# Decoder step on one core: sample queries' memory logits moved from TensorE to GpSimd products and VectorE sums, and a third of the early weight splits moved to GpSimd

## The chip, the core and the metric

The kernel runs on one core of one Trainium2 chip. A core has a matrix engine (TensorE, PE in the profile), a vector engine (VectorE, DVE), a scalar engine (ScalarE, ACT), GpSimd (POOL) and SyncE (SP), which here issues nearly all the DMAs. Each works through its own row of instructions in order and waits for the others by semaphores. Matmul results go to PSUM; all else lies in SBUF. The metric is the device time of one launch in microseconds (us), median of the runs. A change of under 0.2%, 3.3 us here, is about what a measurement of this kernel can't tell from no change.

## The reference, cut to what matters

One layer of a decoder with three parallel branches, for a prompt of 256 tokens and for 8 samples of 4 new tokens each (32 rows), with the same weights. The branch that the change touches is the cross attention of the samples' queries into cached memory keys, 4 heads of 128, 256 keys for each sample:

```python
def memory_attend(q, k, v):
    s = jnp.einsum('bqhd,bmhd->bhqm', q, k).astype(jnp.float32) * (HEAD_DIM ** -0.5)
    p = jax.nn.softmax(s, axis=-1)
    return jnp.einsum('bhqm,bmhd->bqhd', p.astype(v.dtype), v)
...
qm = rms_norm(q_mem.reshape(b, t, MEM_HEADS, HEAD_DIM), p['g_q_mem'])
y_mem = memory_attend(qm, mem_k, mem_v).reshape(b, t, MEM_WIDTH) @ p['w_mem_out']
```

For the samples `mem_k` is `cache_mem_k`, an input. All arithmetic is in float32.

## The kernel before

All weights stand in one array, the wall, as 504 slabs of 128 partitions x 1024 numbers (512 KB), in the order in which they are used. Each slab is loaded by SP into a buffer `wr` (4 of them), rounded by ScalarE to a high half `wh` in the fast matmul format (line 305), and VectorE subtracts that from the original to get the low half `wl` (line 316, "the split"). There are 4 buffers of `wh` and `wl`. TensorE then does, for the 8 blocks of a slab, three products of 128x128 by 128x288: high by high and low activations, low by high activations (`products`, line 488): 24 matmuls a slab. The 288 columns are 256 prompt tokens and 32 sample rows.

The order of the work on each engine is written when the program is built: every piece of work is a generator that asks for an engine for so many us; a planner (`Order.run`) takes the ask that can start first, by rank where several can, and issues the instructions in that order. Its costs are the functions `dve`, `act`, `pool`, `pe`, `sp`, and nothing is reordered at run time. `main` gives the order of the slabs: memory projection (slabs 0 to 15), the first convolution tiles (16 to 23), the other convolution tiles (24 to 31), the four memory-query heads (`mem_head`, 32 to 39), the eight stick-breaking heads (40 to 87), then gates and branch projections, the output and the MLP.

Of the samples' memory attention (`samples`): the queries of all four heads are spread by VectorE into a zeroed tile `qmx` of 32 columns for each head and sample, so that each sample's columns are zero outside its own four rows. Eight loads bring the keys `mkc`, transposed on the host, 512 KB for each sample. TensorE multiplies in 32 steps (line 1033) and adds all up in one PSUM tile `zm` (128 rows: head x sample row; 256 keys). Softmax and the products with the values follow, then the stick-breaking samples (`sb_sample`).

GpSimd has little to do before: it zeroes tiles, multiplies the convolution windows of the samples (line 706, 992 elements, four times), and in the last two thirds adds and squares tiles of 288 columns (lines 1332 and 1346). VectorE also runs the convolution's 31 taps for each of four tiles (line 719), the norms of the heads (lines 814 to 832, 434 to 438) and the splits of activations (843).

Of the kernel before, what the change touches and what calls it, by code (L numbers as in the profile page):

```python
# [14 lines left out]
P = 128  # L15
# [136 lines left out]


def dve(n, *flags, **take):
    return Ask("DVE", 0.18 + n / 920.0, flags, **take)


def act(n, *flags, **take):
# [17 lines left out]
PAD = 64  # L176
SHIFT = 5
VISIT, VISIT_K = 4, 8
MM = 0.131
MM_MEM = 0.226  # L180

# [2 lines left out]
def tile_decoder_step(ctx: ExitStack, tc: tile.TileContext, xT, memT, wall, cvec, kmat, ptab,  # L184
# [124 lines left out]
    def sub_part(s, i):  # L309
        sl = slabs[s]  # L310
        n = SLAB // sl.parts
        yield dve(n, late=Order.HOP + 0.1)
        if i == 0:
            sl.l = shifted("wl", s)
        c = slice(i * n, (i + 1) * n)
        nc.vector.tensor_sub(sl.l[:, c], sl.raw[:, c], sl.h[:, c].bitcast(F32))  # L316
        done(sl.split[i])
        if i == sl.parts - 1:
            give("wr")
# [559 lines left out]
    qmx = []  # L879

    def mem_head(h):
        def evac(ps):
            box = []
            yield from head_norm(ps, C_GQM, box, Flag())
            q = box[0]
            if h == 0:
                yield pool(1024, k4=1)
                qmx.append(tl("k4", [P, MH, NB, NS]))
                nc.gpsimd.memset(qmx[0], 0.0)
            yield dve(NS, *([qm_made[0]] if h else []))  # L890
            spread(nc, qmx[0][:, h], q[:, NP:])
# [12 lines left out]
            yield pe(0.5, pa=1)  # L904
            tp = bank("pa")
            for m in range(2):
                for a in range(2):
                    nc.tensor.transpose(tp[:, m * NP + a * P:m * NP + (a + 1) * P],  # L908
                                        p[:, a * ML + m * P:a * ML + (m + 1) * P], ident)
# [90 lines left out]
    def sample_values(load, aex, psum, x_T, new, first, cost):  # L1000
# [18 lines left out]
            give("k4")  # L1019
        give("k4", 2)  # L1020

    def samples():

        tiles, flags = [], [Flag() for _ in range(NB)]
        yield sp(qm_made[0])
        add(load_tiles(mem_tiles(mkc, [P, MH, ML]), tiles, flags, range(NB)), 2)
        for b in range(NB):
            if b % VISIT_K == 0:
                yield pe(VISIT_K * 0.5, *flags[b:b + VISIT_K], *qm_made, **({} if b else {"pl": 1}))
            if b == 0:  # L1030
                zm = bank("pl")[:, :ML]
            for h in range(MH):
                nc.tensor.matmul(zm[h * NS:(h + 1) * NS, :], qmx[0][:, h, b, :], tiles[b][:, h, :],  # L1033
                                 start=(b == 0), stop=(b == NB - 1))
            give("k4")
        give("k4")
        yield dve(0, *om_made, s=1)
        p = tl("s", [P, 512])[:, :ML]
        yield from softmax_rows(zm, 1, p)
        give("pl")  # L1040
# [372 lines left out]
    def main():  # L1413
        yield from warm_up()
        yield from mem_products()
        yield from conv_products([evac_lin(0, "pa"), evac_gat(0, "pa"), evac_lin(1, "pm"), evac_gat(1, "pm")])
        for j in range(2, CT):
            yield from main_tile(hx, evac_lin(j, "pm"))
            yield from main_tile(hx, evac_gat(j, "pm"))
        add(samples(), 3.0)  # L1420
        for h in range(MH):
            yield from main_tile(hx, mem_head(h), 2 + 0.05 * h)
        for h in range(SH):
            yield from main_tile(hx, sb_key(h), 2.2 + 0.05 * h)
            yield from main_tile(hx, sb_query(h), 2.2 + 0.05 * h)
# [55 lines left out]
def _layout(inp):  # L1481
# [38 lines left out]
    for k2 in range(KT // 2):  # L1520
        r = slice(2 * k2 * P, (2 * k2 + 2) * P)
        put_rows(np.concatenate([w_in[r, j * P:(j + 1) * P] for j in (0, CT, 1, CT + 1)], 1))
    for j in range(2, CT):
        put(w_in, j)
        put(w_in, CT + j)
    for h in range(MH):
        put(w_in, m0 + h)
    for h in range(SH):
        put(w_in, k0 + h)
        put(w_in, q0 + h)  # L1530
# [12 lines left out]
    for c in range(4):  # L1543
# [30 lines left out]
    n_pool = a["cache_sb_k"].shape[1]  # L1574
    ck = a["cache_sb_k"][0].reshape(n_pool, P, 2, 4, HD)
    cvv = a["cache_sb_v"][0].reshape(n_pool, P, 2, 4, HD)
    return {
        "xT": feat(x),
        "memT": feat(a["mem_prompt"][0]),
# [6 lines left out]
        "mkc": np.ascontiguousarray(a["cache_mem_k"][0].transpose(0, 3, 2, 1)),  # L1586
# [34 lines left out]
```

## Time and profile before

| what | us |
|---|---|
| median of 3 timed runs (1635.0 to 1635.33) | 1635.23 |
| profiled execution, first to last instruction | 1632.5 |
| TensorE busy | 1627.7 |
| VectorE busy | 992.1 |
| ScalarE busy | 739.3 |
| GpSimd busy | 139.1 |

The profiled execution is known by its span; the page gives no other time of its own for it. Engines' busy times overlap and don't add up. In the rows below, a group is written as line, engine, operation, tile written <- tiles read, shapes and count, then busy us, mean ns of one, and the idle time before it with what ended it; a row of the timeline or of the chain begins with its start and length in us from the start of the span. A tile that is called `k` in the profile is one of the pool `k4` (9 tiles of 1024 columns). `pm`, `pa` and `pl` are PSUM tiles.

### The profile page before, as it was taken

The numbers are of one execution on the slowest core, as the hardware profiler recorded it, in microseconds if no ns is written. First come the engines' busy times: TensorE is split into PE (matmuls) and PEld (weight loads), VectorE is DVE, ScalarE is ACT, GpSimd is POOL, SyncE is SP. The second block draws the span as 40 slices with busy tenths as digits, with TensorE's granted clock in tenths as the row PEclk, the third lists the DMA queues.
The fourth block names the chain that finished last, engine by engine and source line by source line (L and its number), as shares of the span: only waits on it lengthen the run. The fifth ranks groups of instructions, "written<-read, shape, count | busy, mean of one in ns | idle before, by whom it ended". The sixth has DMA issues, their size and how long they took to land.

```text
span 1632.5 us, 30962 instructions
## 1 busy us (share of the span) xinstructions
PE 1627.7 (100%) x12786; PEld 1610.3 (99%) x12786; DVE 992.1 (61%) x1471; ACT 739.3 (45%) x1070; POOL 139.1 (9%) x104
## 2 busy tenths in 40 slices
PE   9999999999999999999999999999999999999999
PEld 7999999999999999999999999999999999999999
DVE  8889888877677655565555544455445554455443
ACT  8746766644444534444443333333333333333332
POOL 0020000000000000001222200121001210022100
PEclk9999999999999999999999999999999999999999
DMA  9787465777755555546655555555555555555563
GB/s 339 217 186 251 153 209 189 248 257 252 254 166 169 163 179 167 174 153 212 191 176 168 169 168 168 169 169 174 165 173 170 168 170 169 168 168 168 180 194 99
DMA packets 107103, 305.39 MB, mean 187 GB/s; under 512 B 19922, under 2 KB 29522, under 8 KB 106962
## 3 DMA queue, kind: packets, MB, share of 16 engines
q1 hardware_dynamic: 106818, 303.39, 58.2%
q8 instruction: 100, 1.64, 0.4%
q14 instruction: 41, 0.34, 0.1%
q10 hardware_dynamic: 144, 0.02, 0.0%
HBM read 297.05 MB, written 6.32 MB: 186 GB/s over the span
## 4 chain that ended last, share of the span: by engine, by line
PE 99%; DMA 0%; SPq 0%; ACT 0%; DVE 0%; issue 0%
PE pm L488 93%; PE pm L541 3%; PE pa L488 1%; PE pl L1017 1%; PE pl L1190 0%; PE pa L854 0%; PE pa L855 0%; PE pa L853 0%; DMA wr<-in_wall 0%; PE pl L1033 0%; PE pa L827 0%; PE pa L1144 0%; PE pa L908 0%; PE pa L1141 0%; PE pa L1143 0%; PE pa L1107 0%
## 5 line engine op out<-in xcount | busy, mean ns | idle before, releaser
L305 ACT CAST wh<-wr 128x1024 fp32r<-128x1024 f32 (+1 forms) x520 | 530.3, 1022 | 648.1 <-PE pm L488 597.0
L488 PE MATMUL pm<-a,wh 128*128 128x288 f32 x5184 | 739.1, 293 | 0.0
L316 DVE TENSOR_TENSOR wl<-wr,wh 128x1024 fp32r<-128x1024 f32 (+1 forms) x520 | 617.2, 1190 | 195.2 <-ACT wh L305 190.5
L488 PEld LDWEIGHTS pm<-a,wh 128*128 128x128 f32 x5184 | 696.7, 188 | 1.3 <-issue 1.2
L488 PE MATMUL pm<-a,wl 128*128 128x288 f32 x2592 | 397.0, 292 | 0.0
L488 PEld LDWEIGHTS pm<-a,wl 128*128 128x128 f32 x2592 | 358.4, 188 | 0.0
L488 PE MATMUL pm<-k,wh 128*128 128x288 f32 x2160 | 306.7, 292 | 0.0
L488 PEld LDWEIGHTS pm<-k,wh 128*128 128x128 f32 x2160 | 290.2, 188 | 0.0
L488 PE MATMUL pm<-k,wl 128*128 128x288 f32 x1120 | 171.6, 292 | 0.0
L488 PEld LDWEIGHTS pm<-k,wl 128*128 128x128 f32 x1120 | 155.1, 188 | 0.0
L1346 POOL TENSOR_TENSOR t<-t 128x288 f32<-128x288 f32 x64 | 96.7, 1511 | 599.5 <-DVE t L1343 599.5
L1360 DVE TENSOR_TENSOR a<-a,pm 128x288 f32<-128x288 f32 x64 | 29.0, 454 | 122.4 <-PE pm L488 122.4
L1343 DVE SCALAR_TENSOR_TENSOR t<-pm,rx 128x288 f32<-128x288 f32 x64 | 29.2, 457 | 90.4 <-PE pm L488 90.4
L1349 ACT CAST k<-t 128x288 fp32r<-128x288 f32 x56 | 24.1, 433 | 115.6 <-POOL t L1346 115.6
L1262 DVE TENSOR_TENSOR t<-pm,rx 128x288 f32<-128x288 f32 x48 | 22.0, 458 | 71.5 <-PE pm L488 71.5
L488 PE MATMUL pm<-s,wh 128*128 128x288 f32 x400 | 65.1, 292 | 0.0
L719 DVE SCALAR_TENSOR_TENSOR a<-a,cv,a 128x256 f32<-128x256 f32 x120 | 57.5, 480 | 1.4
L1332 POOL TENSOR_TENSOR t<-t,t 128x288 f32<-128x288 f32 x15 | 21.6, 1441 | 419.3 <-ACT t L1329 419.3
L488 PEld LDWEIGHTS pm<-s,wh 128*128 128x128 f32 x400 | 56.6, 188 | 0.0
L1351 DVE TENSOR_TENSOR k<-t,k 128x288 fp32r<-128x288 f32 x52 | 23.8, 458 | 51.1 <-ACT k L1349 51.1
L541 PE MATMUL pm<-wh,a 128*128 128x512 f32 x128 | 34.6, 391 | 0.2 <-ACT wh L305 0.2
L488 PE MATMUL pm<-s,wl 128*128 128x288 f32 x160 | 33.8, 292 | 0.0
(212 smaller groups left out, 784.4 us busy)
## 6 DMA issues: line engine op xcount, KB each, us to landing
wr<-in_wall SPq DMA_DIRECT2D x488, 512.0 KB, 3.6
wr<-in_wall SPq DMA_DIRECT2D x32, 256.0 KB, 4.8
k<-in_kpool SPq DMA_DIRECT2D x32, 256.0 KB, 5.9
k<-in_vpool SPq DMA_DIRECT2D x32, 256.0 KB, 5.8
k<-in_mkc SPq DMA_DIRECT2D x8, 512.0 KB, 10.2
k<-in_mvc SPq DMA_DIRECT2D x8, 512.0 KB, 6.5
t<-in_xT SPq DMA_DIRECT2D x16, 144.0 KB, 3.7
out_yT<-a SPq DMA_DIRECT2D x16, 144.0 KB, 1.9
```

The lines of the kernel that those rows point to most:

```text
L305: nc.scalar.copy(sl.h[:, c], sl.raw[:, c])
L316: nc.vector.tensor_sub(sl.l[:, c], sl.raw[:, c], sl.h[:, c].bitcast(F32))
L488: nc.tensor.matmul(ps, w, a, start=(first and i == 0), stop=(last and i == len(todo) - 1))
L541: nc.tensor.matmul(ps[m], y[:, m * P:(m + 1) * P], z[:, w], start=(k == 0 and j < 2), stop=(k == KT - 1 and j in (4, 5)))
L719: nc.vector.scalar_tensor_tensor(c[:, :NP], up[:, k:k + NP], w, c[:, :NP], op0=ALU.mult, op1=ALU.add)
L1262: nc.vector.tensor_mul(g, ps, rx)
L1332: nc.gpsimd.tensor_add(sq_sum[0], sq_sum[0], res[0])
L1343: nc.vector.scalar_tensor_tensor(r, ps, 0.0, r2, op0=ALU.max, op1=ALU.mult)
L1346: nc.gpsimd.tensor_mul(r, r, r)
L1349: nc.scalar.copy(a.h, r)
L1351: nc.vector.tensor_sub(a.l, r, a.h.bitcast(F32))
L1360: nc.vector.tensor_add(x1[j], x1[j], ps)
```

## The change

Four things change.

1. The samples' logits leave TensorE. The keys now lie with 128 partitions of (sample, a quarter of 32 keys, head): `lane_loads` brings 8 tiles of 128 x 8 x 128, 512 KB each, of which the first two are loaded at once and each further one when the tile two before it is used up. `lane_queries` copies the queries on GpSimd to a tile in which each query row stands four times, TensorE transposes it four times, ScalarE copies it out of PSUM. `lane_products` multiplies on GpSimd each key tile by each of the four queries (32 products of 1024 elements), and for each product VectorE sums over the 128 elements of a head (`lane_sum`); a product waits for the sum two before it. `lane_rows` brings the logits back into the former layout by VectorE transposes of 32 x 32 blocks.
2. Of the slabs 24, 27, ... 108 (`LENT`, 29 of them) GpSimd makes the low half instead of VectorE.
3. The memory-query heads come before the convolution tiles 2 and 3, in the program and in the wall.
4. The planner's costs of VectorE and GpSimd are changed. With all this the planner makes a new order for every engine.

The diff, cut:

```diff
 def dve(n, *flags, **take):
-    return Ask("DVE", 0.18 + n / 920.0, flags, **take)
+    return Ask("DVE", 0.17 + n / 1004.0, flags, **take)
...
 def pool(n, *flags, **take):
-    return Ask("POOL", 0.3 + n / 420.0, flags, **take)
+    return Ask("POOL", 1.0 + n / 580.0, flags, **take)
...
+LANES = 8
+LENT = range(24, 110, 3)
...
     def sub_part(s, i):
         sl = slabs[s]
         n = SLAB // sl.parts
-        yield dve(n, late=Order.HOP + 0.1)
+        other = s in LENT
+        yield (pool if other else dve)(n, late=Order.HOP + 0.1)
...
-        nc.vector.tensor_sub(sl.l[:, c], sl.raw[:, c], sl.h[:, c].bitcast(F32))
+        (nc.gpsimd if other else nc.vector).tensor_sub(sl.l[:, c], sl.raw[:, c], sl.h[:, c].bitcast(F32))
...
-            if h == 0:
-                yield pool(1024, k4=1)
-                qmx.append(tl("k4", [P, MH, NB, NS]))
-                nc.gpsimd.memset(qmx[0], 0.0)
-            yield dve(NS, *([qm_made[0]] if h else []))
-            spread(nc, qmx[0][:, h], q[:, NP:])
+            yield act(NS)
+            nc.scalar.copy(qs[:, h, :], q[:, NP:])
...
+    def lane_loads(cache, tiles, got, used):
+        for c in range(LANES):
+            yield sp(*([used[c - 2]] if c >= 2 else []), k4=1)
+            t = tl("k4", [P, LANES, HD])
+            nc.sync.dma_start(t, cache[c])
...
+    def lane_queries(q, made, x):
+        yield pool(512, *made, s=1)
...
+        nc.gpsimd.tensor_copy(x[0].rearrange("p q (r a) -> p q r a", a=4), v)
+        yield pe(0.45, pa=1)
+        tp = bank("pa")
+        for i in range(NQ):
+            nc.tensor.transpose(tp[:, i * HD:(i + 1) * HD], x[0][:, i, :], ident)
+        yield act(512)
+        nc.scalar.copy(x[0].rearrange("p q d -> p (q d)"), tp)
...
+    def lane_sum(prod, out, flag):
+        yield dve(LANES * prod.shape[-1])
+        nc.vector.reduce_sum(out, prod, axis=AX.X)
+        give("k4")
+        done(flag)
...
+        for c in range(LANES):
+            for q in range(NQ):
+                yield pool(1024, got[c], *flags[-2:-1], k4=1)
+                prod = tl("k4", [P, LANES, HD])
...
+                nc.gpsimd.tensor_mul(prod, tiles[c], y)
...
+                add(lane_sum(prod, part, flags[-1]), 1.5)
+            give("k4")
+            done(used[c])
...
+    def lane_rows(z, out):
+        yield dve(ML, a=1)
+        t = tl("a", [P, T])[:, :ML]
+        nc.vector.transpose(t, z)
...
-        add(load_tiles(mem_tiles(mkc, [P, MH, ML]), tiles, flags, range(NB)), 2)
-        for b in range(NB):
...
-            for h in range(MH):
-                nc.tensor.matmul(zm[h * NS:(h + 1) * NS, :], qmx[0][:, h, b, :], tiles[b][:, h, :],
-                                 start=(b == 0), stop=(b == NB - 1))
...
+        add(lane_loads(mkc, tiles, got, used), 2)
+        yield from lane_queries(qs[:, :MH, :].rearrange("p h r -> p (h r)"), qm_made, x)
+        yield from lane_products(tiles, got, used, x[0], out)
+        yield from lane_rows(out[0], out)
...
+        add(samples(), 3.0)
+        for h in range(MH):
+            yield from main_tile(hx, mem_head(h), 2 + 0.05 * h)
         for j in range(2, CT):
             yield from main_tile(hx, evac_lin(j, "pm"))
             yield from main_tile(hx, evac_gat(j, "pm"))
-        add(samples(), 3.0)
-        for h in range(MH):
-            yield from main_tile(hx, mem_head(h), 2 + 0.05 * h)
```

The lines after line 178 move: what was line 316 is 321, 706 is 711, 719 is 724, 814 to 832 are 819 to 837. The new order is shown at three places; a row is line, operation, tile written <- tiles read, size, and a number in a tile's name is its serial number.

**VectorE, around slabs 46 and 47.** Before, ten rows in which the splits (L316) of slabs 47, 48 and 49 stand:

```order
L316 TENSOR_TENSOR wl_2092<-wr_1918,wh_2032 128x1024
L1472 COPY k_296_1773<-a_2075 128x8x4
L824 TENSOR_TENSOR t_1992<-t_1991,t_1992 64x288
L814 TENSOR_TENSOR t_2115<-pm_1927,rx 128x288
L316 TENSOR_TENSOR wl_2126<-wr_1955,wh_2083 128x1024
L862 TENSOR_REDUCE sm_108<-pa_2103 128x2
L864 TENSOR_SCALAR sm_108<-sm_108 128x2
L843 TENSOR_TENSOR a_2113<-a_2075,a_2112 128x256
L820 TENSOR_TENSOR t_2116<-t_2116 64x288
L316 TENSOR_TENSOR wl_2172<-wr_2021,wh_2162 128x1024
```

Now, the first passage of the prediction, with the splits (L321) of slabs 46 and 47:

```order
L1046 TENSOR_REDUCE a_1892<-k_350_2032 128x8
L915 TENSOR_TENSOR s_2069<-pa_2052,s_2068 128x512
L825 TENSOR_TENSOR t_2058<-t_2058 64x288
L321 TENSOR_TENSOR wl_2100<-wr_1997,wh_2082 128x1024
L1046 TENSOR_REDUCE a_1892<-k_361_2072 128x8
L829 TENSOR_TENSOR t_2059<-t_2058,t_2059 64x288
L929 TENSOR_TENSOR a_2128<-pa_2111,a_2127 128x256
L819 TENSOR_TENSOR t_2151<-pm_2034,rx 128x288
L321 TENSOR_TENSOR wl_2156<-wr_2002,wh_2130 128x1024
L825 TENSOR_TENSOR t_2152<-t_2152 64x288
L724 SCALAR_TENSOR_TENSOR a_1338<-a_1249,cv,a_1338 128x256
L867 TENSOR_REDUCE sm_108<-pa_2165 128x2
```

The sums L1046 have come between, and every third split has gone. L915, L929 and L819 read PSUM; L825, L829, L724 and the splits read SBUF tiles alone.

**VectorE, around slabs 52 and 53.** Before:

```order
L316 TENSOR_TENSOR wl_2368<-wr_2164,wh_2343 128x1024
L870 RECIPROCAL sm_110<-sm_109 128x2
L824 TENSOR_TENSOR t_2317<-t_2316,t_2317 64x288
L814 TENSOR_TENSOR t_2402<-pm_2291,rx 128x288
L719 SCALAR_TENSOR_TENSOR a_1426<-a_1356,cv,a_1426 128x256 x3
L1129 SCALAR_TENSOR_TENSOR s_2381<-s_2379,s_2380 128x384
L1131 TENSOR_TENSOR s_2381<-s_2381,km 128x2x128
L820 TENSOR_TENSOR t_2403<-t_2403 64x288
L316 TENSOR_TENSOR wl_2460<-wr_2177,wh_2434 128x1024
```

Now, the second passage of the prediction:

```order
L825 TENSOR_TENSOR t_2402<-t_2402 64x288
L819 TENSOR_TENSOR t_2437<-pm_2345,rx 128x288
L321 TENSOR_TENSOR wl_2449<-wr_2299,wh_2390 128x1024
L321 TENSOR_TENSOR wl_2465<-wr_2311,wh_2423 128x1024
L724 SCALAR_TENSOR_TENSOR a_1338<-a_1249,cv,a_1338 128x256
L1186 SCALAR_TENSOR_TENSOR s_2434<-s_2432,s_2433 128x384
L1046 TENSOR_REDUCE a_1892<-k_437_2460 128x8
L1188 TENSOR_TENSOR s_2434<-s_2434,km 128x2x128
L829 TENSOR_TENSOR t_2403<-t_2402,t_2403 64x288
L825 TENSOR_TENSOR t_2438<-t_2438 64x288
L1159 TENSOR_TENSOR a_2522<-pm_2442,rx 128x288
L1046 TENSOR_REDUCE a_1892<-k_442_2496 128x8
```

Two splits now stand one behind the other, with one sum between the taps and the stick-breaking head's rows, and another at the end.

**GpSimd, same part of the program.** Before, the convolution's four products and memsets are all that stands there:

```order
L706 TENSOR_TENSOR k_245_1427<-a_1341,cv 128x992
L706 TENSOR_TENSOR k_251_1465<-a_1343,cv 128x992
L706 TENSOR_TENSOR k_256_1497<-a_1396,cv 128x992
L687 MEMSET a_1562 128x30
L706 TENSOR_TENSOR k_279_1648<-a_1552,cv 128x992
L889 MEMSET k_296_1773 128x1024
```

Now, from the product whose sum opens the first passage:

```order
L1063 TENSOR_TENSOR k_350_2032<-k_263_1498,s_1817 128x1024
L1063 TENSOR_TENSOR k_361_2072<-k_266_1511,s_1817 128x1024
L321 TENSOR_TENSOR wl_2109<-wr_1890,wh_2041 128x1024
L1063 TENSOR_TENSOR k_373_2143<-k_266_1511,s_1817 128x1024
L1063 TENSOR_TENSOR k_383_2187<-k_266_1511,s_1817 128x1024
L1063 TENSOR_TENSOR k_385_2217<-k_266_1511,s_1817 128x1024
L321 TENSOR_TENSOR wl_2255<-wr_2043,wh_2198 128x1024
```

A lent split (slab 45 is `wl_2109`, 48 is `wl_2255`) stands behind every two or three products. In all, GpSimd's row now has 29 splits and 32 products more, nearly all the products between slabs 42 and 71.

More of the change, by code (lines that the diff above doesn't have):

```diff
@@ L1020, in sample_values @@
         give("k4", 2)
+    def lane_loads(cache, tiles, got, used):
[3 more added lines that the diff above has]
+            nc.sync.dma_start(t, cache[c])
+            tiles.append(t)
+            got[c].at = order.landed(524) + 1.0
+    def lane_queries(q, made, x):
+        yield pool(512, *made, s=1)
+        x.append(tl("s", [P, NQ, HD]))
+        v = bass.AP(tensor=q.tensor, offset=q.offset, ap=[list(q.ap[0]), [1, NQ], [NQ, NS], [0, 4]])
+        nc.gpsimd.tensor_copy(x[0].rearrange("p q (r a) -> p q r a", a=4), v)
[5 more added lines that the diff above has]
+        nc.scalar.copy(x[0].rearrange("p q d -> p (q d)"), tp)
+        give("pa")
@@ new lines, in lane_sum, with lane_products @@
+    def lane_sum(prod, out, flag):
[3 more added lines that the diff above has]
+        done(flag)
+    def lane_products(tiles, got, used, x, out):
+        yield dve(0, a=1)
+        z = tl("a", [P, T])[:, :ML]
+        out.append(z)
+        z = z.rearrange("p (q k) -> p q k", q=NQ)
+        flags = []
+        for c in range(LANES):
+            for q in range(NQ):
+                yield pool(1024, got[c], *flags[-2:-1], k4=1)
+                prod = tl("k4", [P, LANES, HD])
+                y = x[:, q, :]
+                y = bass.AP(tensor=y.tensor, offset=y.offset, ap=[list(y.ap[0]), [0, LANES], [1, HD]])
+                nc.gpsimd.tensor_mul(prod, tiles[c], y)
+                flags.append(Flag())
+                part = z[:, q, c * LANES:(c + 1) * LANES]
+                add(lane_sum(prod, part, flags[-1]), 1.5)
+            give("k4")
+            done(used[c])
+        yield dve(0, *flags[-2:])
+        give("s")
@@ L1022, in samples @@
+    def lane_rows(z, out):
+        yield dve(ML, a=1)
+        t = tl("a", [P, T])[:, :ML]
+        nc.vector.transpose(t, z)
+        yield dve(ML)
+        for i in range(2):
+            v = bass.AP(tensor=t.tensor, offset=t.offset + 32 * i, ap=[list(t.ap[0]), [1, 4], [NQ, NB], [64, NQ]])
+            nc.vector.transpose(z.rearrange("p (a i k) -> p i a k", a=4, i=2)[:, i], v)
+        give("a")
+        out.append(z)
     def samples():
-        tiles, flags = [], [Flag() for _ in range(NB)]
+        x, out = [], []
@@ L1036, in samples @@
-        give("k4")
+        tiles, got, used = [], [Flag() for _ in range(LANES)], [Flag() for _ in range(LANES)]
+        add(lane_loads(mkc, tiles, got, used), 2)
+        yield from lane_queries(qs[:, :MH, :].rearrange("p h r -> p (h r)"), qm_made, x)
+        yield from lane_products(tiles, got, used, x[0], out)
+        yield from lane_rows(out[0], out)
+        zm = out[1]
         yield dve(0, *om_made, s=1)
@@ L1039, in samples @@
         yield from softmax_rows(zm, 1, p)
-        give("pl")
+        give("a")
         aex, om = [], []
@@ L1522, in _layout @@
         put_rows(np.concatenate([w_in[r, j * P:(j + 1) * P] for j in (0, CT, 1, CT + 1)], 1))
+    for h in range(MH):
+        put(w_in, m0 + h)
     for j in range(2, CT):
@@ L1525, in _layout @@
         put(w_in, CT + j)
-    for h in range(MH):
-        put(w_in, m0 + h)
     for h in range(SH):
@@ L1576, in _layout @@
     cvv = a["cache_sb_v"][0].reshape(n_pool, P, 2, 4, HD)
+    mk = a["cache_mem_k"][0].reshape(NB, 4, LANES, LANES, MH, HD)
     return {
```

8 lines of the change are left out of this document (1 added, 7 removed).

## The prediction

> **What bounds the kernel now.** I read the page first (busy shares, then the chain that ended last), then the chain in order of time, then the groups of each engine.
>
> ```profile
> span 1632.5 us, 30962 instructions
> PE 1627.7 (100%) x12786; PEld 1610.3 (99%) x12786; DVE 992.1 (61%) x1471; ACT 739.3 (45%) x1070; POOL 139.1 (9%) x104
> PE 99%; DMA 0%; SPq 0%; ACT 0%; DVE 0%; issue 0%
> ```
>
> TensorE (PE) is busy all through the span, and 99% of the chain is PE behind PE: nothing that PE waits for costs anything today. So only two things can move the time: work taken from PE or given to it, and new waits of PE. The span is 1632.5 us; the median of the timed runs is 1635.23, so 2.7 us lie around the span, and I add them again at the end.
>
> ```profile
> 79.55 36.66 PE pm L488 x282
> 147.49 3.59 PE pl L1033 x64
> 154.07 0.44 PE pa L908 x4
> ```
>
> These rows of the chain (start, length, what) give PE's prices. 36.66 us for 282 weight products is 0.130 us for one, so a slab of 24 takes 3.12 us, and PE asks for a new slab that often. L1033 is what the change removes, L908 are four transposes of the kind that it adds.
>
> That averages hide a stage is seen in the windows. I cut at the slabs: 24 to 41, 42 to 71 and 72 to 95 of the weight wall, since the change works there.
>
> ```profile
> 75.20:132.80 57.60, 57.60 (x446) 57.60 (x445) 51.56 (x84) 30.73 (x44) 11.77 (x6) 1.00 0.85 204
> 132.80:249.30 116.50, 116.50 (x990) 114.31 (x989) 99.90 (x191) 79.75 (x165) 2.86 (x3) 1.00 0.60 209
> 249.30:340.80 91.50, 91.50 (x800) 89.42 (x799) 76.25 (x147) 58.23 (x116) 1.90 (x2) 1.00 0.64 222
> ```
>
> Columns: PE, PE loads, VectorE (DVE), ScalarE, GpSimd (POOL), clock, DMA share, GB/s. Over the whole span DVE is at 61%, but in these stages at 90%, 86% and 83%. The granted clock is 1.00 and stays out of it; the DMA share in the middle stage is 0.60.
>
> **What is taken from PE.** L1033 with its 3.59 us goes; 0.09 more was lost at the change to it (an estimate: the same hand-over costs 0.08 at L908). Four transposes come: 0.44 and 0.08. PE's work falls by 3.68 - 0.52 = 3.2 us, 0.2% of the span. ScalarE copies of 32 columns replace VectorE's spreads of 32 columns, both about 0.2 us and off PE's path: nothing. The eight loads of 512 KB are as many as before. If nothing else happened, the median would be 1632.0.
>
> **What GpSimd and VectorE get.** In slabs 24 to 109 GpSimd gets 29 splits and 32 products of 1024 elements, and VectorE 32 sums over 1024 in place of the 29 splits.
>
> ```profile
> L316 DVE TENSOR_TENSOR wl<-wr,wh 128x1024 fp32r<-128x1024 f32 x488 | 596.1, 1223 | 192.9 <-ACT wh L305 188.4 <-ACT t L1329 1.5 <-DMA wr<-in_wall 1.3
> L709 DVE TENSOR_REDUCE a<-k 128x32 f32<-128x992 f32 x4 | 4.7, 1173 | 0.0
> L719 DVE SCALAR_TENSOR_TENSOR a<-a,cv,a 128x256 f32<-128x256 f32 x120 | 57.5, 480 | 1.4
> L843 DVE TENSOR_TENSOR a<-a,a 128x256 fp32r<-128x256 f32 x28 | 11.3, 417 | 0.2 <-ACT a L841 0.2
> L820 DVE TENSOR_TENSOR t<-t 64x288 f32<-64x288 f32 x20 | 9.1, 454 | 0.6
> L1135 DVE SCALAR_TENSOR_TENSOR s<-s,s 128x384 f32<-128x384 f32 x8 | 4.4, 550 | 0.0
> L862 DVE TENSOR_REDUCE sm<-pa 128x2 f32<-128x512 f32 x4 | 2.7, 686 | 1.2 <-PE pa L855 1.2
> L706 POOL TENSOR_TENSOR k<-a,cv 128x992 f32<-128x992 f32 x4 | 10.8, 2712 | 61.6 <-DVE a L692 61.5
> ```
>
> By busy time alone it is an exchange: 29 splits of 1.22 leave (35.4), 32 sums of 1.17 come (37.4). The price lies in the two engines' getting in each other's way. The four GpSimd products of the kernel before (L706) show it in order of time:
>
> ```profile
> 92.75 2.38 POOL L706 TENSOR_TENSOR k<-a,cv 128x992 f32<-128x992 f32 x1 [50.75 <-DVE a L692]
> 95.10 3.19 POOL L706 TENSOR_TENSOR k<-a,cv 128x992 f32<-128x992 f32 x1
> 98.41 2.20 POOL L706 TENSOR_TENSOR k<-a,cv 128x992 f32<-128x992 f32 x1
> 111.43 3.08 POOL L706 TENSOR_TENSOR k<-a,cv 128x992 f32<-128x992 f32 x1 [10.75 <-DVE a L692]
> ...
> 94.40 0.46 DVE L662 TENSOR_TENSOR a<-pm,rx 128x288 f32<-128x288 f32 x1 [1.30 <-PE pm L488]
> 94.78 1.44 DVE L316 TENSOR_TENSOR wl<-wr,wh 128x1024 fp32r<-128x1024 f32 x1
> 96.14 2.20 DVE L692 TENSOR_TENSOR a<-a,a 128x32 f32<-128x32 f32 x1
> 98.26 1.17 DVE L709 TENSOR_REDUCE a<-k 128x32 f32<-128x992 f32 x1
> 99.47 1.25 DVE L712 TENSOR_SCALAR a<-a,cv 128x32 f32<-128x32 f32 x1
> 111.27 1.22 DVE L316 TENSOR_TENSOR wl<-wr,wh 128x1024 fp32r<-128x1024 f32 x1
> 112.52 2.31 DVE L824 TENSOR_TENSOR t<-t,t 64x288 fp32r<-64x288 f32 x1
> ```
>
> Read them in pairs. The split at 111.27 was running when the product came at 111.43: the split takes its usual 1.22, and the product ends at 114.51, 2.02 after the split's end. The next DVE instruction, L824, begins at 112.52 inside the product and takes 2.31 where 0.45 is usual: it ends just after the product. L692 on 32 elements takes 2.20 inside the product of 95.10 and ends with it (98.34 against 98.29). So a VectorE instruction that reads two SBUF tiles and a GpSimd product exclude each other, and the one that comes second waits for the whole of the first; a tiny one-tile scalar op (L712) waited too. The sum L709 at 98.26 keeps its 1.17 although the product of 98.41 runs beside it, and L662, which reads a PSUM tile (pm) and one SBUF tile, its 0.46 inside the first product. And GpSimd, once waiting, gets in at the next border between two VectorE instructions (at 96.22, ahead of L692). A product holds VectorE off for 2.02 to 2.20; by 1024/992 I take 2.1 for the splits and products of the change. [...]
>
> **Price of one GpSimd instruction.** Passages of the new order, shown with the change, let it be worked out by hand: VectorE's rows in turn, GpSimd's beside them, a two-tile row waits while GpSimd holds, PSUM readers and sums don't, GpSimd takes the next border, and a product waits for the sum two before it.
> First passage (slabs 46 and 47), GpSimd's product k_361 starting with the first row: the sum and L915 end at 1.86, L825 waits to 2.10 (0.24) and runs to 2.55, the lent split of slab 45 holds to 4.65, the split of slab 46 waits 2.10, L829 after the next sum waits 0.93, the split of slab 47 waits 1.23. The rows take 8.86 us busy and 13.4 in all: 4.5 of waiting over 4 GpSimd instructions, 1.1 for each.
> Second passage (slabs 52 and 53), same rules: the split of slab 52 waits 1.65, that of 53 2.10, L829 and L825 2.10 each: 8.0 us over 4, 2.0 for each.
> The mean is 1.56. Bounds: none under 0, since nothing in the rows makes a waiting engine faster; 2.1 with nothing beside it.
>
> **The sum by stages.** The new order has in slabs 42 to 71 on VectorE 20 splits, 28 sums and 106 others, on GpSimd 10 lent splits and 29 products. The others come to 0.40 each: in the middle window of before, 99.90 less 30 splits (36.6) is 63.3 for 158. VectorE: 24.4 + 32.8 + 42.4 = 100; the waits: 39 x 1.56 = 61; together 161. PE has there 720 products (93.8) and 88 small ones at 0.11 to 0.17 (10.6, an estimate from L908's 0.11 each and the 0.130 above): 104.4. PE falls behind by 57.
> Slabs 24 to 41: 12 splits, 2 sums, 81 others are 49, 10 GpSimd instructions add 16; PE has 61.7: +3. Slabs 72 to 95: 16 splits, 2 sums, 155 others (0.37, many of them tiny) are 79, 11 GpSimd instructions add 17; PE has 91.5 as before: +5. Slabs 96 to 109 carry 5 lent splits among little else: nothing.
> The weights stand up to three slabs ahead of PE (four buffers), 9 us: so much is eaten before PE first waits, and it doesn't come back as time.
> -3 + 57 + 3 + 5 - 9 = +53: the span 1685.5, the median **1688**.
>
> Bounds. If VectorE's sums and PSUM readers always lay beside GpSimd, only the excluding work would have to fit: splits 24.4, 72 others 28.8 and 39 times 2.06 are 133.5, against 104.4: +29, less 9 and 3, 1652. At 2.0 each (the second passage all over) and no cover from the buffers: 74 + 8 + 12 - 3 = +91, 1726. GpSimd's copy of 512 (L1035), VectorE's three 32 x 32 transposes and the four buffers' refill are not in the trace before; each comes once: under 0 nothing speaks for a gain, and above I bound them together by two products, 6 us; I take 0. [...]
>
> **Rivals.**
> *The waits are covered* (ends on the other side). VectorE has 104.4 - 100 = 4 us to spare in the middle stage and 9 in the buffers, 13 over 39: if a GpSimd instruction costs VectorE less than 0.34, PE never waits and only the 3.2 us show: 1632.0, on the border of what a measurement can tell from no change (0.2%, 3.3 us). For it: 32 sums stand beside the products, and DVE's average is 61%. Against it: L692, L712 and L824, and both passages.
> *Packing is nearly ideal*: 1636 to 1650, when the buffers stretch further than three slabs.
> *GpSimd's row is late by itself.* A lent split stands behind products in GpSimd's row (slab 45's after slab 46's on VectorE), a product waits for a sum, and VectorE's sums wait for products; on SP the loads of later lanes wait for lanes used up, with weight loads behind them. If these rings add up, every GpSimd instruction costs more than 2.1: 0.4 more for 39 is 16, 1726 to 1750.
>
> **How the numbers follow.** Forecast with its bounds 0.79; covered 0.11, half on each side of the 0.2% line; nearly ideal 0.04; late rings 0.06. The range 1650 to 1726 holds the first. Faster 0.05, same 0.06, slower 0.89.
>
> **What would show it.** PE's chain should have gaps between 133 and 300 us that end on VectorE's low halves (wl), VectorE near 100% busy there with splits of 1.5 to 2.5 us on average in place of 1.22, GpSimd products of 2.7 to 3.3, sums at 1.2. After slab 109 every row should be as before, only later. If VectorE's splits stay at 1.22 in that stage, the exclusion doesn't bind and I am wrong; if they are long but PE has no gap, the cover was larger than I took; if PE waits for GpSimd's wl instead, it is the last rival.

## The result and the profile after

| kernel | median us | range | ratio to before |
|---|---|---|---|
| before | 1635.28 | 1635.0 to 1635.44 | |
| changed | 1704.0 | 1702.83 to 1705.17 | 1.0422 [1.0409, 1.0434] |

The changed kernel is 4.2% slower. The forecast was 1688 in a range of 1650 to 1726. The page of the changed kernel, with the busy shares and then the rows of 40 slices (tenths of each slice; PEclk is the granted clock):

```profile
span 1703.2 us, 30935 instructions
PE 1650.2 (97%) x12726; PEld 1628.3 (96%) x12726; DVE 1088.3 (64%) x1473; ACT 745.1 (44%) x1079; POOL 282.5 (17%) x165
PE   9997787899999999999999999999999999999999
DVE  8899999998777665556555554455444554455543
PEclk9998788999999999999999999999999999999999
```

The damage lies in slices 4 to 8 (each 42.6 us), where PE is at 7 and 8 tenths and VectorE at 9. From there to the end PE is full again. The 96 us more on VectorE's busy line, 1088.3 against 992.1, are the first thing to explain, since by instruction counts the change is an exchange.

Cut at the slabs, the first three stages as in the prediction: 24 to 41, 42 to 71, 72 to 95 and 96 to 109, where the changed kernel has them (columns PE, PE loads, VectorE, ScalarE, GpSimd, clock, DMA share, GB/s):

```profile
76.60:140.30 63.70, 62.35 (x480) 61.76 (x479) 58.70 (x80) 37.03 (x66) 27.90 (x16) 1.00 0.69 165
140.30:304.30 164.00, 124.55 (x810) 120.18 (x809) 162.65 (x164) 67.35 (x125) 95.42 (x39) 0.84 0.41 126
304.30:407.40 103.10, 96.41 (x808) 94.56 (x809) 99.19 (x180) 63.29 (x132) 24.42 (x14) 0.97 0.62 206
407.40:460.75 53.35, 53.35 (x556) 50.64 (x555) 43.69 (x76) 26.64 (x38) 12.14 (x7) 1.00 0.74 265
```

In the second row VectorE works 162.65 of 164.00 us, and GpSimd only 95.42: VectorE, idle for 1.35 us in all, is what fills the stage; in the third row it is idle for 3.91. Slab 110 begins at 460.75 in place of 390.09, 70.7 later, and that distance stays to the end.

The groups of the changed kernel that answer to those of before (mean ns of one is the second number behind the bar):

```profile
L321 DVE TENSOR_TENSOR wl<-wr,wh 128x1024 fp32r<-128x1024 f32 x459 | 573.9, 1252 | 194.4 <-ACT wh L309 194.2
L1046 DVE TENSOR_REDUCE a<-k 128x8 f32<-128x1024 f32 x32 | 38.7, 1209 | 0.1
L724 DVE SCALAR_TENSOR_TENSOR a<-a,cv,a 128x256 f32<-128x256 f32 x120 | 76.2, 635 | 1.7
L825 DVE TENSOR_TENSOR t<-t 64x288 f32<-64x288 f32 x20 | 20.7, 1035 | 0.7
L1213 DVE TENSOR_TENSOR s<-s,s 128x384 fp32r<-128x384 f32 x8 | 9.7, 1207 | 0.0
L819 DVE TENSOR_TENSOR t<-pm,rx 128x288 f32<-128x288 f32 x20 | 8.8, 450 | 1.2 <-PE pm L493 1.1
L1063 POOL TENSOR_TENSOR k<-k,s 128x1024 f32<-128x1024 f32 x32 | 85.2, 2688 | 2.8 <-ACT s L1041 2.8
L321 POOL TENSOR_TENSOR wl<-wr,wh 128x1024 fp32r<-128x1024 f32 x29 | 62.2, 2146 | 270.1 <-ACT wh L309 235.9 <-DVE a L948 14.3 <-PE pm L493 11.4
```

Sort them by what they read. L825 reads SBUF alone: 1035 ns where the row of before (L820) had 454. The taps L724 went from 480 to 635. L819 reads PSUM and keeps 450 (452 as L814 before); the sums L1046 keep 1.2 us. A mean over the whole span dilutes it: most of the 459 splits lie outside these stages and take 1.23 us on average, so that 1252 looks harmless. Cut to slabs 42 to 95, where 38 of them lie, the split takes this:

```profile
L321 DVE TENSOR_TENSOR wl<-wr,wh 128x1024 fp32r<-128x1024 f32 x38 | 58.0, 1528 | 0.1
L724 DVE SCALAR_TENSOR_TENSOR a<-a,cv,a 128x256 f32<-128x256 f32 x24 | 19.2, 801 | 0.2
```

What PE waited for in the changed kernel, in us, times and the longest:

```profile
PE pa L859 <- DVE s L1213: 12.1, 4, 5.3
PE pa L908 <- ACT s L878: 10.9, 2, 8.2
PE pa L1200 <- DVE s L1195: 6.3, 3, 3.7
PE pa L1164 <- DVE a L1159: 5.5, 2, 4.4
PE pa L832 <- DVE t L829: 5.3, 3, 3.1
```

None of PE's waits in these slabs names a low half `wl`. Every row shown is of a small matmul of an attention head (`pa` in PSUM), whose input comes late from a chain over VectorE and ScalarE. The longest one, with the rows around it of four engines one after the other (PE, VectorE, GpSimd, ScalarE), each in order of time:

```profile
150.23 1.30 PE L908 MATMUL pa<-km,s 128*128 128x128 f32 x4 [8.20 <-ACT s L878]
...
138.37 2.67 DVE L724 SCALAR_TENSOR_TENSOR a<-a,cv,a 128x256 f32<-128x256 f32 x1
140.96 0.41 DVE L929 TENSOR_TENSOR a<-pa,a 128x256 fp32r<-128x256 f32 x1
141.29 2.25 DVE L724 SCALAR_TENSOR_TENSOR a<-a,cv,a 128x256 f32<-128x256 f32 x1
143.47 1.21 DVE L1046 TENSOR_REDUCE a<-k 128x8 f32<-128x1024 f32 x1
...
144.99 0.68 DVE L867 TENSOR_REDUCE sm<-pa 128x2 f32<-128x512 f32 x1
...
135.81 7.45 POOL L1063 TENSOR_TENSOR k<-k,s 128x1024 f32<-128x1024 f32 x3
...
149.66 0.91 ACT L878 ACTIVATE s<-s,sm 128x256 f32<-128x256 f32 x2
```

PE made the scores of a memory head at 133.2. The maximum over them, L867, stands in VectorE's row behind two taps that the three GpSimd products (135.81 to 143.26) stretch from 0.48 to 2.67 and 2.25 us, behind a sum and a third tap; it starts at 144.99. (Just before them L697, on 32 elements, had taken 2.39 us from 136.05.) ScalarE's exponentials and L878 follow, and PE goes on after 8.20 us of idling.

### The profile page after: what moved, and what is told of

It reads as the page before. It is cut to its first block, busy times and chain, and to the rows that moved or that the text cites. A ratio compares the mean times of both kernels' runs of the same rounds, so it can differ in the third digit from the quotient of the medians.

```text
span 1703.2 us, 30935 instructions
## 1 busy us (share of the span) xinstructions
PE 1650.2 (97%) x12726; PEld 1628.3 (96%) x12726; DVE 1088.3 (64%) x1473; ACT 745.1 (44%) x1079; POOL 282.5 (17%) x165
## 4 chain that ended last, share of the span: by engine, by line
PE 79%; DVE 1%; issue 1%; DMA 0%; POOL 0%; ACT 0%; DVEq 0%; POOLq 0%; ACTq 0%
PE pm L493 77%; PE pl L1017 0%; PE pl L1247 0%; DMA wr<-in_wall 0%; DVE a L724 0%; DVE wl L321 0%; DVE s L1213 0%; POOL wl L321 0%; PE pa L859 0%; PE pa L860 0%; DVE a L848 0%; DVE t L441 0%; PE pa L858 0%; DVE t L439 0%; DVE s L1203 0%
## 5 line engine op out<-in xcount | busy, mean ns | idle before, releaser
L493 PE MATMUL pm<-a,wh 128*128 128x288 f32 x5184 | 752.1, 296 | 0.8 <-ACT qs L1141 0.7
L321 DVE TENSOR_TENSOR wl<-wr,wh 128x1024 fp32r<-128x1024 f32 (+1 forms) x491 | 594.9, 1215 | 196.9 <-ACT wh L309 196.5
L493 PEld LDWEIGHTS pm<-a,wh 128*128 128x128 f32 x5184 | 708.5, 191 | 3.1 <-issue 1.9
L493 PE MATMUL pm<-a,wl 128*128 128x288 f32 x2592 | 402.4, 295 | 0.0
L493 PEld LDWEIGHTS pm<-a,wl 128*128 128x128 f32 x2592 | 363.7, 190 | 0.4 <-issue 0.4
L321 POOL TENSOR_TENSOR wl<-wr,wh 128x1024 fp32r<-128x1024 f32 x29 | 62.2, 2146 | 270.1 <-ACT wh L309 235.9
L1063 POOL TENSOR_TENSOR k<-k,s 128x1024 f32<-128x1024 f32 x32 | 85.2, 2688 | 2.8 <-ACT s L1041 2.8
L724 DVE SCALAR_TENSOR_TENSOR a<-a,cv,a 128x256 f32<-128x256 f32 x120 | 76.2, 635 | 1.7
```

Source lines behind the costliest of these rows:

```text
L321: (nc.gpsimd if other else nc.vector).tensor_sub(sl.l[:, c], sl.raw[:, c], sl.h[:, c].bitcast(F32))
L493: nc.tensor.matmul(ps, w, a, start=(first and i == 0), stop=(last and i == len(todo) - 1))
L724: nc.vector.scalar_tensor_tensor(c[:, :NP], up[:, k:k + NP], w, c[:, :NP], op0=ALU.mult, op1=ALU.add)
L1063: nc.gpsimd.tensor_mul(prod, tiles[c], y)
```

## The experiments

Two theories were set against each other. **A, exclusion**: a VectorE instruction with two SBUF inputs and a GpSimd instruction that reads SBUF shut each other out, each GpSimd instruction costs VectorE some 1.5 us, and VectorE's total sets the end. **B**: something else in the change is dear: the new order of the program, GpSimd's row and its waits for sums and loads, or the lower clock. The kernel before was run on the same chip each time, at close to 1635.1, and the ratios are to that.

**The same order, but GpSimd reads nothing** (logits and a third of the early low halves are left out):

```diff
-        (nc.gpsimd if other else nc.vector).tensor_sub(sl.l[:, c], sl.raw[:, c], sl.h[:, c].bitcast(F32))
+        if other:
+            nc.gpsimd.memset(sl.l[:, c].bitcast(F32), 0.0)
+            nc.gpsimd.memset(sl.l[:, c].bitcast(F32), 0.0)
+        else:
+            nc.vector.tensor_sub(sl.l[:, c], sl.raw[:, c], sl.h[:, c].bitcast(F32))
...
-                nc.gpsimd.tensor_mul(prod, tiles[c], y)
+                nc.gpsimd.memset(prod, 0.01)
+                nc.gpsimd.memset(prod, 0.02)
```

> Each of the 32 GpSimd products and 29 lent splits becomes two memsets of the same tile (1.9 us, by 0.95 for a memset of 1024 in the profile before): GpSimd's row, its waits and everybody's order stay, but it reads no SBUF there. The logits and a third of the early low halves are left out. Theory A (GpSimd's reads and VectorE's two-tile instructions exclude each other): VectorE gets its 61 us of waiting back, splits return to 1.22 us, and the time is 1632 to 1642. Theory B (the new order or GpSimd's latency in its own right makes PE wait): 1690 to 1710 as in the changed kernel.

Measured: 1633.05 us, ratio 0.9988 [0.9978, 0.9998]. From its page, and its window from 150 to 200 us behind it:

```profile
span 1630.9 us, 30987 instructions
PE 1625.5 (100%) x12726; PEld 1609.5 (99%) x12726; DVE 995.3 (61%) x1473; ACT 745.3 (46%) x1079; POOL 249.6 (15%) x226
```

```profile
150.00:200.00 50.00, 50.00 (x390) 49.96 (x389) 46.63 (x77) 31.81 (x61) 34.71 (x38) 1.00 0.57 187
```

GpSimd is busier in this window than in the changed kernel (34.71 against 29.71), all the sums are there, and so are GpSimd's waits for free tiles, and PE is full. What GpSimd doesn't do here is wait for what it would read: ScalarE's high halves, the loads of the keys. That these waits are not the cause is seen in the changed kernel itself: no wait of PE in these slabs names GpSimd, and VectorE is hardly idle in the stage that loses. VectorE has the same 1473 instructions in the same order and is busy for 995.3 us in place of 1088.3. So 93.0 us of VectorE's busy line are waiting, and they come from what GpSimd reads; over 61 GpSimd instructions that is 1.52 us for each. In the run without reads, where 61 pairs of memsets only write, the 459 splits of 1024 elements take 1223 ns on average, as the 488 of before did: in them no waiting shows.

**The order alone**: before, with the heads moved ahead of the convolution tiles and the planner's new costs.

```diff
-    return Ask("DVE", 0.18 + n / 920.0, flags, **take)
+    return Ask("DVE", 0.17 + n / 1004.0, flags, **take)
...
-        for j in range(2, CT):
...
         for h in range(MH):
             yield from main_tile(hx, mem_head(h), 2 + 0.05 * h)
+        for j in range(2, CT):
```

> The kernel before with the memory heads put before the convolution tiles and the new planner costs, nothing else. Theory A: PE stays without gaps, 1634 to 1638. Theory B (the order, planned with VectorE costs that are too low, is what costs): 1660 or more.

Measured: 1636.39 us, 1.0008 [0.9999, 1.0018]. The moved heads and costs by themselves are worth nothing that can be measured.

**Each half alone.** First the changed kernel without the lent splits, then the kernel before with them (and with GpSimd's new planner cost):

```diff
-LENT = range(24, 110, 3)
+LENT = ()
```

```diff
-        nc.vector.tensor_sub(sl.l[:, c], sl.raw[:, c], sl.h[:, c].bitcast(F32))
+        (nc.gpsimd if other else nc.vector).tensor_sub(sl.l[:, c], sl.raw[:, c], sl.h[:, c].bitcast(F32))
```

> The changed kernel with no split lent to GpSimd, all on VectorE. Theory A: each lent split costs VectorE about 1.56 us of waiting and saves it 1.22, so giving all 29 back brings 10 us: 1690 to 1697. Rival (the splits' lateness on GpSimd is what PE waits for): 1640 to 1660. Rival (lending relieves VectorE as meant): 1715 to 1740.

> The kernel before with the 29 splits lent to GpSimd (and its planner cost raised), nothing else. Theory A: 29 times 1.56 less 1.22 is 10 us more for VectorE, spread over stages where it has 10 to 17% to spare: 1635 to 1641. If lending by itself makes PE wait: 1650 or more.

Measured: 1692.19 us, 1.0351 [1.0333, 1.0368], and 1638.54 us, 1.0022 [1.0012, 1.0031]. Both lie in A's brackets. In the changed kernel the lent splits cost 11.8 us (1704.0 against 1692.19). In the order of before they cost some 3.5 us, but not because they cost VectorE little: the page of that run says 1002.8 us busy, where before less 29 splits of 1.223 would be 956.6: 46.2 over 29 is again 1.59 us for each. There a lent split saves VectorE 1.22 and costs it 1.59, and VectorE had room for the difference.

**Each half blind**: in the changed kernel, the products become memsets while the lent splits are read (the logits are left out), then the other way about (a third of the early low halves is left out), with the two memsets of the first experiment each time.

> The changed kernel with the 32 products as pairs of memsets (the logits are left out), the 29 lent splits as they are. Theory A by its prices: the sums' busy time fits, as the run without reads showed, and 29 splits at 1.56 less 1.22 add 10 us of VectorE's time spread over 86 slabs: 1634 to 1644. If a lent split costs much more than that: 1655 or more.

> The changed kernel with the 29 lent splits as pairs of memsets (a third of the early low halves is left out as zero), the 32 products as they are. Theory A: in slabs 42 to 71 VectorE has 100 us of work and 29 products at 1.56 to 1.6 of waiting, 146, against 104 on PE: 1670 to 1690. If products and splits only hurt together: 1650 or less.

Measured: 1646.26 us, 1.0072 [1.0055, 1.0089], two us over the upper end given for it, and 1678.73 us, 1.027 [1.0253, 1.0287], within its bracket. Over the 1633.05 of the run that reads nothing, the lent splits cost 13.2 us of time and the products 45.7, together 58.9 of the 71.0; the last 12 come only where both are there. That a full row has no room for either would explain it; no run shows it by itself.

**Half the products**: only two of the four query rows of a sample are multiplied (half of the logits is left out, and their tile is zeroed first).

```diff
-            for q in range(NQ):
+            for q in range(0, NQ, 2):
```

> The changed kernel with 16 products and 16 sums instead of 32 (two of each sample's four query rows are left out, their logits are zero). They stand at the same density over half the slabs, so by theory A half of the loss goes: 1665 to 1675. A loss from a fixed cause (a late start, the order at one place): 1690 or more.

Measured: 1674.55 us, 1.0238 [1.0221, 1.0255], at the upper end of A's bracket. With all the lent splits in place, 0, 16 and 32 products lose 13.2, 41.5 and 71.0 us over the run that reads nothing: each half of the products costs nearly the same, so no fixed cause holds the loss.

**Is it the clock?** In the changed kernel the granted clock falls to 0.50 for short stretches (below). Here PE gets three idle matmuls of 288 columns ahead of each small group of the heads (`fill`, 156 matmuls in all, some 20 us of PE), so that it stands still less.

```diff
+    def fill(ps):
+        for _ in range(3):
+            nc.tensor.matmul(ps[:, :T], ones_r, hx[0].h, start=True, stop=True)
```

> The changed kernel with three idle 288-column matmuls ahead of 52 of the small PSUM groups of the heads, into the same PSUM tile, which the real ones overwrite: 156 times 0.13, 20 us more for PE, in the rows where it waits; all other rows as in the changed kernel. Theory A (VectorE is the bound there, PE's lower granted clock only fills its waits): 1702 to 1712. If PE's lowered clock is what costs, filling keeps it up: 1685 to 1699. If PE is the bound: 1720 to 1726.

Measured: 1710.2 us, 1.046 [1.0443, 1.0478]. Its row for 150 to 200 us beside that of the changed kernel, changed kernel first:

```profile
150.00:200.00 50.00, 39.96 (x238) 38.03 (x239) 49.55 (x49) 21.95 (x43) 29.71 (x12) 0.78 0.40 125
```

```profile
150.00:200.00 50.00, 41.41 (x255) 39.89 (x256) 49.55 (x49) 21.34 (x41) 29.76 (x12) 0.81 0.38 122
```

VectorE again does 49 instructions in 49.55 us. PE's busy line grew by 15.1 us (1665.3 against 1650.2) and the time by 6.2: PE had room for most of the filler in its waits, so PE's own work is not what sets the end in these stages. The filler raised the clock too little (0.78 to 0.81) to show what a full clock would do. What speaks against the clock as the cause is VectorE's row: with 1.35 us idle in slabs 42 to 71 it leaves a faster PE next to nothing to win there.

**Is it an order that was planned too early?** The planner doesn't know of the waiting. Here it is told: 1.6 us more on VectorE's next free time after each product and each lent split. The second run has the same without lent splits.

```diff
                 nc.gpsimd.tensor_mul(prod, tiles[c], y)
+                order.free["DVE"] += 1.6
```

> The changed kernel with one difference: the planner that orders the program adds 1.6 us to VectorE's next free time after each GpSimd product and after each lent split, so that it plans with the waiting that the trace of the changed kernel shows. All work is done. Theory A (VectorE's total, work and waiting together, is the bound of slabs 24 to 96; no order of TensorE's row can shorten it): 1688 to 1706 us, VectorE still about 99% busy between 100 and 350 us. Rival (the loss is an order planned too early: TensorE's small matmuls stand in its row before their inputs can be ready, and a plan that knows of the waiting heals that): 1650 to 1670 us. Between 1670 and 1688 both have a part.

> The same booking of 1.6 us, here after the products alone, and no split is lent to GpSimd; all work is done. Without the booking this variant took 1692.2 us. Theory A (VectorE's total is the bound): 1678 to 1694 us. Rival (an order planned too early): 1640 to 1660 us.

Measured: 1691.93 us, 1.0349 [1.033, 1.0367], and 1689.69 us, 1.0334 [1.0315, 1.0352]. Both times are in A's bracket, but A's picture of the first is not there. Its window from 150 to 200 us and its longest waits of PE:

```profile
150.00:200.00 50.00, 18.96 (x121) 17.62 (x119) 38.71 (x34) 13.45 (x25) 50.00 (x21) 0.69 0.40 136
```

```profile
PE pm L495 <- DVE t L821: 29.5, 2, 21.3
PE pa L910 <- ACT s L880: 20.9, 1, 20.9
```

With VectorE planned as slow, the planner set most of the products one behind the other (18 of the 32 in this window). For 50 us GpSimd is the full engine (21 instructions, 50.00), VectorE is at 38.71 and spends part of that on sums, and PE stands. The bunch is cheap for VectorE: 1050.8 us busy, 55.5 above the run that reads nothing, 0.91 for each GpSimd instruction: 19 sums lie beside the next product here and don't wait (1212 ns on average), and for 11.29 of the 50 us VectorE has nothing to do and so nothing to hold up. But the serial row of GpSimd takes its place as the bound of this stretch: VectorE's sums wait 9.3 us for products, GpSimd for nothing. Knowing the price saved 12 us; it didn't heal the change.

**Spread out.** If bunching starves PE, even spacing might be free: the planner adds 2.0 us to GpSimd's next free time after each product, so that about two are planned beside three slabs, from 42 to 88. The second run spreads by 3.0 and books VectorE's 1.6 as well.

```diff
                 nc.gpsimd.tensor_mul(prod, tiles[c], y)
+                order.free["POOL"] += 2.0
```

> The changed kernel with one difference: the planner adds 2.0 us to GpSimd's next free time after each product, so that the 32 products stand evenly, about two for three slabs, beside slabs 42 to 88, in place of one for each slab of 42 to 71. All work is done. VectorE's rows of slabs 24 to 95 are 228 us without waiting, TensorE's 258. Theory A (VectorE's total of work and waiting is the bound, a GpSimd instruction costs it 1.1 to 1.6 us wherever its row is full): 228 + 60 x 1.1 to 1.6 = 294 to 324, so 1668 to 1697 us. Rival (the price is one of density: spread out, a GpSimd instruction costs VectorE as little as in the lent splits alone, at most 0.45 us): 1632 to 1645 us. Between them the price lies between.

> Products spread by 3.0 us on GpSimd's next free time, and 1.6 us booked on VectorE after each product and each lent split, so that TensorE's row is planned for the waiting and GpSimd's row holds no long run of products. All work is done. Theory A: as the spread kernel or some us less, 1660 to 1690 us. Rival (density): 1632 to 1645 us. Over 1695 us the booking itself makes a worse order.

Measured: 1733.86 us, 1.0603 [1.0586, 1.0621], and 1746.69 us, 1.0681 [1.0663, 1.0699]: far above the brackets of A and of the rival. The second lies where its expectation has the booking make a worse order; no further run tests that. In the first run, the price is not what failed. Its VectorE is busy for 1092.6 us, 97.3 above the run that reads nothing, 1.60 for each GpSimd instruction: spreading makes them no cheaper. What is new is in VectorE's groups in slabs 42 to 95:

```profile
L321 DVE TENSOR_TENSOR wl<-wr,wh 128x1024 fp32r<-128x1024 f32 x38 | 54.0, 1420 | 2.6 <-ACT wh L309 2.5
L724 DVE SCALAR_TENSOR_TENSOR a<-a,cv,a 128x256 f32<-128x256 f32 x57 | 49.4, 867 | 1.0
```

57 taps stand there in place of 24 (the row shown with the result), 49.4 us in place of 19.2. PE doesn't need them before the last of the branches. Of these 30.2 us, the 33 taps more at their usual 0.48 are 15.8; the rest is waiting, which in the changed kernel fell on other rows (over the span it is 97.3 us against 93.0). VectorE is busy in these slabs for 283.28 us in place of 261.84, and the slabs take 295.2 in place of 267.1, close to the 29.9 us that this kernel is slower than the changed one. So a longer row of VectorE is some 21 of 28 us, and the rest is time in which VectorE stands idle (11.9 in place of 5.3). The likely reading is that the planner saw gaps on VectorE, which were the waiting that it didn't know of, and filled them with the convolution. That is argued, not shown: no run holds the taps back, and the run with half of the products has 52 of them in these slabs and yet lost less. Why the second run is slower still isn't settled: it has fewer taps there (25), VectorE's waiting is 92.0 us, and VectorE itself idles behind ScalarE for part of the stage.

## Why the prediction was right, and where it was not

- *The mechanism* was right: the run without reads gives the whole loss back (1633.05 us), and L825 (1035 ns against 454 before), the taps (801 in slabs 42 to 95 against 480) and the splits (1528 against 1223) stretch, while PSUM readers and sums keep their times (L819 450 ns, L1046 1209). Its path to PE was not as told (below).
- *The price* of 1.56 us for each GpSimd instruction measured 1.52 over 61 of them (93.0 us). That it came so close was in part luck, since neither of the two passages went as worked out by hand. By the usual 0.45 and 1.22, the first waits for 6.2 us in place of 4.5 (first four rows), the second for 3.8 in place of 8.0: there GpSimd stood still until ScalarE's high half came, and both splits ran at their usual length. The two errors go opposite ways and cancel in part: by what the passages measured, the mean over the eight would have been 1.25.

```profile
154.67 2.29 DVE L825 TENSOR_TENSOR t<-t 64x288 f32<-64x288 f32 x1
157.05 3.26 DVE L321 TENSOR_TENSOR wl<-wr,wh 128x1024 fp32r<-128x1024 f32 x1
161.46 1.40 DVE L829 TENSOR_TENSOR t<-t,t 64x288 fp32r<-64x288 f32 x1
163.60 2.60 DVE L321 TENSOR_TENSOR wl<-wr,wh 128x1024 fp32r<-128x1024 f32 x1
196.56 2.35 DVE L321 TENSOR_TENSOR wl<-wr,wh 128x1024 fp32r<-128x1024 f32 x2
201.26 2.15 DVE L829 TENSOR_TENSOR t<-t,t 64x288 fp32r<-64x288 f32 x1
203.44 2.54 DVE L825 TENSOR_TENSOR t<-t 64x288 f32<-64x288 f32 x1
200.74 2.36 POOL L321 TENSOR_TENSOR wl<-wr,wh 128x1024 fp32r<-128x1024 f32 x1 [7.06 <-ACT wh L309]
```

- *The price is not a constant.* In the changed order with the products blind a lent split cost VectorE 1.23 (1030.9 us busy, 35.6 more than without reads, over 29), with the splits blind a product 1.61; the lent splits in the order of before gave 1.59, the spread run 1.60, bunched products 0.91.
- *The middle stage.* The run without reads shows how long the new order takes PE when nothing waits: slabs 42 to 71 lie between 137.62 and 242.05 us, 104.4. The changed kernel took 164.0. Forecast +57, measured +59.6; VectorE forecast at 161 us, measured 162.65. Compared instruction by instruction with the run without reads, VectorE waits there for 60.8 us, where 39 times 1.56 is 61. (A small slip lies in the upper bound: at 2.0 each, slabs 72 to 95 would give 9.5, not 12, and the bound moves by some 3 us.)
- *The neighbours.* Against that same run, slabs 24 to 41 gave +2.0 (forecast +3), 72 to 95 +10.0 (forecast +5), 96 to 109 nothing (forecast nothing). The second was undersized by 5. For slabs 24 to 41 VectorE waits 16.4 us more, and PE loses only 2.0 of it there; the next point says where the rest went.
- *The cover by the weight buffers* is the step that failed: "The weights stand up to three slabs ahead of PE (four buffers), 9 us: so much is eaten before PE first waits". VectorE did fall behind before PE waited for long, but nothing was saved by it. When PE begins slab 42, VectorE has begun 203 instructions, in the run without reads 218; when PE begins slab 72, it is 366 against 369. What was borrowed was paid back inside the middle stage, as time. And the four buffers cover the splits alone. PE's row is in order and has the heads' small matmuls in it, which wait for VectorE's norms and softmax with no buffer ahead of them. In the list of PE's waits they are all but 0.7 us of what there is in these stages; no product waited for a low half. (The low halves were not early for that: during the wait of 8.20 us that ends at 150.23, VectorE made that of slab 43, from 147.15 on.) With -9 taken as 0 and +10 for +5 the sum is 1702, and 1704.0 was measured.
- *The gaps that end on `wl`*, foretold under what would show it, are therefore not there; that forecast fell with the step above. The splits' 1.5 to 2.5 us hold at their lower edge within the stages (1.53), GpSimd's products at theirs (2.69 for 2.7 to 3.3).
- *PE's gain of 3.2 us* is covered up, and what shows of it is smaller: the run without reads is 1.9 us faster than before, and its PE line is 2.2 us shorter. The new order by itself cost 1.4 us in the run of the order alone, which would make up the rest; that is not shown.
- *The rivals.* "The waits are covered" fell with the deciding point of 0.34 us against 1.52. "GpSimd's row is late by itself" is not what happened in the changed kernel: no wait of PE in these slabs names GpSimd, and GpSimd is busy for 95.42 of 164.00 us; it did appear once the planner bunched the products. GpSimd's waits for free tiles cost nothing in the run without reads.

What stays open: 24 taps, 19.2 us, stand in slabs 42 to 95 of the changed kernel, and in a full row they may cost about their length. An order that holds them back was not tried. Even so it would end above 1635 if the rest of the 71 us stays. The run without reads, which pays none of the waiting, gained 1.9 us over before.

## What to carry to other kernels

Work moved from VectorE to GpSimd cost nothing here only where GpSimd read nothing (1633.05 us); where it read SBUF beside VectorE instructions with two SBUF tiles, VectorE waited (93.0 us in all). So count the stage's VectorE rows, add what a GpSimd instruction cost VectorE (here 0.9 to 1.6 us for 1024 elements, 1.5 on average), and compare with the bounding engine in that stage, not over the span. A buffer covers only the chain that it stands in, and a lead that is used up in one stage can fall due in the next; look for the other inputs in the bounding engine's row. A planner that counts waiting as free time can fill it with work that isn't due.

## What the runs showed of the hardware that was not expected

The granted clock went down with the waits: it was 0.84 in slabs 42 to 71, where PE was busy for 124.55 of 164.00 us. In the changed kernel it was at 0.50 in nine stretches of 3.4, 6.8 or 10.2 us between 145 and 394 us, 58 us together. One of them between its neighbours, then the last:

```profile
135.00:145.10 10.10, 7.03 (x55) 6.79 (x53) 10.10 (x8) 0.00 (x0) 8.27 (x4) 1.00 0.30 39
145.10:155.40 10.30, 5.17 (x21) 4.96 (x22) 10.23 (x16) 7.39 (x13) 0.75 (x1) 0.50 0.59 190
155.40:172.50 17.10, 13.82 (x105) 13.41 (x104) 16.84 (x17) 6.38 (x13) 13.17 (x6) 1.00 0.30 95
```

```profile
386.00:390.90 4.90, 3.20 (x26) 2.98 (x25) 4.83 (x5) 0.82 (x1) 4.21 (x3) 1.00 0.44 73
390.90:394.30 3.40, 3.40 (x16) 3.40 (x16) 3.36 (x9) 1.99 (x6) 0.00 (x0) 0.50 0.51 112
```

In the last row PE is busy throughout and does 16 matmuls in 3.40 us, 0.21 each, where 0.130 is usual: it pays after the wait. The waiting before it was 1.70 us (386.00 to 390.90 has 3.20 busy of 4.90). The run without reads, with PE busy for 1625.5 of 1630.9 us, has a clock of 1.00 throughout. PE's busy line rose by 24.7 us against that run, but VectorE was idle for only 1.35 us of the middle stage, so most of these 24.7 us lay beside VectorE's row.

A short operation with one input tile waited too. L871, a TENSOR_SCALAR on 128x2, took 1.64 us on average in the window of the booked run shown above, where L877, a RECIPROCAL on 128x2, kept 0.15; L869, the same instruction in the changed kernel, took 0.15 at 147.08, when no product ran.
